# A second norm written out tile by tile over four k-steps, and a latent copied out of PSUM

## The chip, the cores and the metric

The kernel runs on one core of a Trainium2 chip. The metric is the time of one execution on the device in microseconds (us); of several executions the median is taken. The engines of the core run side by side and wait for each other by semaphores: TensorE (PE) multiplies and transposes into PSUM, VectorE (DVE) and ScalarE (ACT) work element by element, GpSimd (POOL) does a few small powers here, and the queue of SyncE (SP) issues the DMAs.

## The reference

Input is one sequence of 256 tokens of width 2048, in float32. A gMLP layer comes first, then one layer of latent attention, each with shift, scale and gate rows computed from a vector c (adaLN):

```python
h = rms_norm(x, norm_g[0]) * (1 + scale) + shift
u, v, z = jnp.split(h @ a_w_in, 3, axis=-1)
y = gelu(u) * mix(layer_norm(gelu(v))) * silu(z)
x = x + gate * (y @ a_w_out)                    # the projection: 4096 -> 2048
...
h_kv = rms_norm(x, kv_norm_g) * (1 + kv_scale) + kv_shift
c_kv, k_r = jnp.split(h_kv @ w_dkv, [512], axis=-1)   # block d: 512 + 64 columns
k_nope, v = heads(rms_norm(c_kv, g_kva) @ w_ukv)
k_rope = rope(rms_norm(k_r, g_kr))
...
h = rms_norm(x, norm_g[1]) * (1 + scale) + shift      # the second norm
c_q, z = jnp.split(h @ b_w_in, [512], axis=-1)        # blocks c (512 columns) and z, y (2 x 1024)
q = heads(rms_norm(c_q, g_qa) @ b_w_uq)
x = x + gate * ((attention(q, k, v) * silu(z)) @ b_w_out)
```

## The kernel before

The 256 tokens are two tiles of 128 (t = 0, 1). Every matrix product is a `Block`: per k-step a 1 MB piece of the weight comes by DMA into a slot of the pool `wraw` (4 slots, shared with the background rows below), and `load_split` splits each half of it into `hi`, a rounded copy made by ACT, and `lo`, the rest, made by DVE (pool `wsp`, 4 slots each). The other factor is split alike, so that a product is three matmuls: hi x hi, lo x hi and hi x lo. A k-step with 1024 columns is 2 halves x 2 tiles x 2 column halves x 3 = 24 matmuls of 512 columns. `drive` goes through the list of steps and issues the preparation of the next step ahead of the matmuls of this one.

`project()` (L630) multiplies with a_w_out in two Blocks of 16 k-steps each, for 1024 columns each. `ev_o` adds the gated result to x (`residual`, L624), and `norm1.chunk` sums the squares and transposes the row chunk into `zT`. In the last step of the second Block, `early1` (L688) runs for each tile: the mean's power on POOL (`rstd_of`, L136), one transpose to spread it over the partitions, the scaling of the first 4 of 16 chunks (L296), and their shift and scale to `h`, split into `gh` on ACT and `gl` on DVE. `late1` (L700) does the other 12 chunks for both tiles at once behind them.

Then `attention()` runs the blocks z and y (b_w_z, 8 k-steps each), d (kv_w_dkv, 8 steps, 288 + 288 columns) and c (b_w_q, 8 steps, 512 columns), all on `mm` banks of PSUM, and keys, queries and heads behind them. `ev_dkv` (L752) closes d: `latent_row` (L711) squares the latent out of PSUM on ACT, gets the power from POOL, and normalises it on ACT from PSUM into `cn`.

In the background the adaLN rows are made: `bg(quota)` adds the quota after each k-step and starts a row (`Ada.step`, L192: 1 MB by DMA into `araw`, one product over 2048 columns on DVE) whenever it has reached 1. The quota is AQ = 0.8 in the projection, until its step STOP = 14, and BQ = 0.9 in z and y, from z's step START = 2.

SP's queue holds the DMAs in the order of the program. The order on the other engines is made by the framework's scheduler, within the data's dependences; `behind(ins)` (L169) places an instruction after a given one.

## Time and profile before

| | us |
|---|---|
| median of 3 runs | 1130.31 |
| lowest, highest | 1128.52, 1131.99 |
| the profiled execution | 1135.89 |
| span of the profiled execution | 1134.2 |
| PE busy in it | 1103.1 |
| DVE busy in it | 952.4 |
| ACT busy in it | 618.4 |

All rows further down come from the profiled execution, whose mean granted TensorE clock was 0.991 of full speed. Its times count from the start of the span. Matmuls are pipelined: the duration of one in a row is longer than the distance to the next, and the distance is what counts. A name in a row is the program's name of a tile: `x` is the residual, `zT` the transposed chunk, `hi` and `lo` the weight's parts, `gh` and `gl` those of h in blocks z, y and c, `shi` and `slo` those in the projection and in d, `araw` a background row, `cn` the latent, `px`, `pm` and `pk` are PSUM tiles.

### The profile page before, as it was taken

What the parts mean: (1) busy time and instruction counts of PE and PEld (TensorE: products, weight loads), DVE (VectorE), ACT (ScalarE), POOL (GpSimd) and SP (SyncE); (2) the same over time, 40 slices, a digit from 0 to 9 for tenths busy, and PEclk for the clock granted to TensorE, in tenths of its full rate; (3) what the DMA queues carried; (4) which work ended last, traced back from release to release, by engine and by line L of the source; (5) the groups of instructions that cost most, each with busy time, mean ns of one, the idle gap of its engine ahead of it and who ended that gap; (6) DMA issues with size and microseconds to landing.
All of it is one profiled execution on the core that took longest, in us unless ns stands there. A gap on an engine that the chain in (4) does not pass through costs nothing.

```text
span 1134.2 us, 14344 instructions
## 1 busy us (share of the span) xinstructions
PE 1103.1 (97%) x5120; PEld 914.8 (81%) x5120; DVE 952.4 (84%) x1379; ACT 618.4 (55%) x1146; POOL 61.6 (5%) x79
## 2 busy tenths in 40 slices
PE   7989999999999999999999999989999999999998
PEld 4877788888888887888888888868889788898876
DVE  5789899989996896897799899869886658779995
ACT  6743445457854435444454455456737579885332
POOL 1000000000310000000000000000000024220000
PEclk8999999999999999999999999998999999999999
DMA  9997889898897988988979989967886645345893
GB/s 347 355 352 269 329 337 364 342 348 307 328 342 289 368 314 304 382 325 326 351 296 357 368 341 376 339 261 280 338 343 207 221 152 185 114 162 214 304 350 122
DMA packets 52330, 340.41 MB, mean 300 GB/s; under 512 B 5889, under 2 KB 6305, under 8 KB 13985
## 3 DMA queue, kind: packets, MB, share of 16 engines
q1 hardware_dynamic: 50402, 335.29, 79.1%
q10 hardware_dynamic: 1152, 2.10, 0.5%
q0 software_dynamic: 704, 2.11, 0.5%
q8 instruction: 40, 0.66, 0.2%
q14 instruction: 32, 0.26, 0.1%
HBM read 337.36 MB, written 2.11 MB: 299 GB/s over the span
## 4 chain that ended last, share of the span: by engine, by line
PE 75%; DVE 9%; DMA 8%; issue 4%; ACT 3%; POOL 0%; DVEq 0%; SPq 0%; ACTq 0%; POOLq 0%
PE pm L341 63%; DMA araw<-in_ada_wT 8%; PE pk L341 4%; DVE lo L167 4%; DVE araw L192 3%; PE pq L341 2%; PE pS L885 1%; PE pS L886 1%; ACT sq L146 1%; ACT hi L165 1%; PE pmix L581 1%; PE px L263 1%; DVE v L481 1%; DMA x<-in_x 0%; PE pT L903 0%
## 5 line engine op out<-in xcount | busy, mean ns | idle before, releaser
L165 ACT CAST hi<-raw 128x1024 fp32r<-128x1024 f32 (+2 forms) x376 | 381.4, 1030 | 379.8 <-PE pm L341 257.0
L167 DVE TENSOR_TENSOR lo<-raw,hi 128x1024 fp32r<-128x1024 f32 (+2 forms) x376 | 442.0, 1195 | 71.4 <-ACT hi L165 68.9
L192 DVE CUSTOM_DVE_ANT_0 araw<-araw,s_b,vec 128x2048 f32<-128x2048 f32 (+1 forms) x128 | 275.1, 2149 | 49.2 <-DMA araw<-in_ada_wT 45.6
L341 PE MATMUL pm<-lo,hh 128*128 128x512 f32 x768 | 249.6, 393 | 4.2 <-DVE lo L167 4.1
L341 PE MATMUL pm<-hi,hh 128*128 128x512 f32 x768 | 242.6, 394 | 8.0 <-ACT hh L302 3.5
L341 PE MATMUL pm<-hi,hl 128*128 128x512 f32 x768 | 247.1, 391 | 0.0
L341 PEld LDWEIGHTS pm<-hi,hh 128*128 128x128 f32 x768 | 144.1, 188 | 41.0 <-ACT hi L165 4.1
L341 PEld LDWEIGHTS pm<-lo,hh 128*128 128x128 f32 x768 | 144.0, 189 | 36.8 <-DVE lo L167 7.4
L341 PEld LDWEIGHTS pm<-hi,hl 128*128 128x128 f32 x768 | 144.6, 188 | 30.3
L341 PE MATMUL pm<-lo,shi 128*128 128x512 f32 (+1 forms) x320 | 94.9, 372 | 0.0
L341 PE MATMUL pm<-hi,slo 128*128 128x512 f32 (+1 forms) x320 | 93.4, 371 | 0.0
L341 PE MATMUL pm<-hi,shi 128*128 128x512 f32 (+1 forms) x320 | 91.1, 373 | 0.0
L341 PEld LDWEIGHTS pm<-hi,shi 128*128 128x128 f32 x320 | 58.2, 188 | 10.1
L341 PEld LDWEIGHTS pm<-lo,shi 128*128 128x128 f32 x320 | 58.3, 188 | 9.9 <-DVE lo L167 0.2
L341 PEld LDWEIGHTS pm<-hi,slo 128*128 128x128 f32 x320 | 58.0, 188 | 10.1
L341 PE MATMUL pm<-hi,gh 128*128 128x512 f32 x160 | 52.7, 404 | 3.1 <-ACT cn L718 2.3
L341 PE MATMUL pm<-hi,gl 128*128 128x512 f32 x160 | 53.4, 400 | 0.0
L341 PE MATMUL pm<-lo,gh 128*128 128x512 f32 x160 | 52.8, 399 | 0.0
L165 ACT CAST shi<-yT 128x512 fp32r<-128x512 f32 x32 | 19.8, 620 | 45.0 <-PE pm L341 44.9
L341 PE MATMUL pm<-hi,ybh 128*128 128x512 f32 x128 | 42.9, 398 | 1.4 <-ACT ybh L165 1.4
L341 PE MATMUL pm<-hi,ybl 128*128 128x512 f32 x128 | 43.1, 399 | 0.0
L341 PE MATMUL pm<-lo,ybh 128*128 128x512 f32 x128 | 43.0, 395 | 0.0
(182 smaller groups left out, 1254.7 us busy)
## 6 DMA issues: line engine op xcount, KB each, us to landing
araw<-in_ada_wT SPq DMA_DIRECT2D x96, 1024.0 KB, 6.8
raw<-in_a_w_in SPq DMA_DIRECT2D x96, 1024.0 KB, 6.9
raw<-in_a_w_out SPq DMA_DIRECT2D x32, 1024.0 KB, 7.2
araw<-in_kv_ada_wT SPq DMA_DIRECT2D x32, 1024.0 KB, 6.9
raw<-in_b_w_z SPq DMA_DIRECT2D x16, 1024.0 KB, 6.2
raw<-in_b_w_out SPq DMA_DIRECT2D x16, 1024.0 KB, 5.9
raw<-in_kv_w_ukv SPq DMA_DIRECT2D x8, 1024.0 KB, 5.0
raw<-in_b_w_uq SPq DMA_DIRECT2D x8, 768.0 KB, 5.0
```

Source lines behind the costliest of these rows:

```text
L146: nc.scalar.activation(j, src, AF.Square, scale=scale, accum_out=dst)
L165: nc.scalar.copy(hi, src)
L167: nc.vector.tensor_tensor(out=lo, in0=src, in1=hi.bitcast(F32), op=ALU.subtract)
L192: nc.vector.tensor_tensor_reduce(out=t[:, c], in0=t[:, c], in1=s_b[:, c], scale=1.0, scalar=acc, op0=ALU.mult, op1=ALU.add, accum_out=dst)
L263: nc.tensor.transpose(p[:, j * P:(j + 1) * P], self.xt[t][:, (q * 4 + j) * P:(q * 4 + j + 1) * P], ident)
L341: nc.tensor.matmul(ps[i][:, :widths[i]], lhsT=lt, rhs=rhs[:, offs[i]:offs[i] + widths[i]], start=(first and c == 0 and which == 0 and rhs ...
L481: nc.vector.tensor_tensor(out=p, in0=ps, in1=p, op=ALU.add)
L581: nc.tensor.matmul(pmix[:, j * 256:(j + 1) * 256], lhsT=wsh["T"][:, g, :], rhs=piece(vt[i], t, n)[:, j * 256:(j + 1) * 256], start=True, s ...
L885: nc.tensor.matmul(pS[:, c0:c1], lhsT=qT[:, j, t * P:(t + 1) * P], rhs=kT[:, j, 0:nk], start=True, stop=False)
L886: nc.tensor.matmul(pS[:, c0:c1], lhsT=qrT[:, t * P:(t + 1) * P], rhs=krT[:, j, 0:nk], start=False, stop=True)
```

## The change

- **The seam.** `early1` and the last step of the second projection Block give way to `passage()`, which covers the last two steps of the projection (14 and 15) and the first two of z, in one written order. A wrapper around the engines, `Engines.keep("order")`, places every instruction of ACT, DVE and PE after the one that was written before it; `keep("behind")` places the later ones after the last of these. Step 15's weight is cast first, and z's step 0 into two slots of its own (`zw0`, `zw1`). Then come the matmuls: tile 0 of steps 14 and 15, tile 1 of step 14 and the first columns of 15, tile 0's broadcast, tile 1's other columns, z's steps 0 and 1 for tile 0 with tile 1's broadcast between, and z's steps 0 and 1 for tile 1. Block z starts at step 2 afterwards.
- **Background rows.** STOP goes from 14 to 12: two rows less are started in the projection's end. BQ goes from 0.9 to 1.0: one row per step in z and y. From z's first weights to the first step of d, 13 rows of the latent's norm and one of the last gate are started, where before there are 11 and two; the other row of the last gate moves to the keys and queries.
- **late1.** The scaling of each further four chunks is placed behind the `gl` of the second chunk of the four before, where before all stand behind the last of `early1`.
- **The latent.** `latent_row` copies the latent (288 + 224 columns), and `ev_dkv` the rotary key (64), from PSUM to SBUF on DVE; squares, power and scaling follow from there (`normalise`). The same holds for the query latent (512 columns) after c. Block d has tail = 1: its last step runs tile by tile, and tile 0 is closed before tile 1's matmuls.

```diff
-BQ = 0.9
+BQ = 1.0
-STOP = 14
+STOP = 12
...
+class Engine:
+    def __init__(self, tc, engine):
+        self.tc, self.engine, self.last, self.mode = tc, engine, None, None
+    def __getattr__(self, name):
+        f = getattr(self.engine, name)
+        if not self.mode:
+            return f
+        def call(*args, **kw):
+            with self.tc.issue_after(self.last.ins) if self.last else nullcontext():
+                ins = f(*args, **kw)
+            if self.mode == "order":
+                self.last = ins
+            return ins
+        return call
+class Engines:
+    def __init__(self, tc):
+        self.sync, self.gpsimd = tc.nc.sync, tc.nc.gpsimd
+        self.scalar, self.vector, self.tensor = (Engine(tc, e) for e in (tc.nc.scalar, tc.nc.vector, tc.nc.tensor))
+    def keep(self, mode):
+        for e in (self.scalar, self.vector, self.tensor):
+            e.mode, e.last = mode, e.last if mode else None
...
-        with behind(chain.pop(0) if chain and queue[0] else None):
-            nc.vector.tensor_tensor(out=lo, in0=src, in1=hi.bitcast(F32), op=ALU.subtract)
+        rest(src, hi, lo)
+    def rest(src, hi, lo):
+        nc.vector.tensor_tensor(out=lo, in0=src, in1=hi.bitcast(F32), op=ALU.subtract)
-    hold, queue, chain = [None], [False], []
+    hold = [None]
...
-            yield from b.items(AQ, tail=TAIL, after=early1 if i else None, then=late1 if i else None, before=fetch, stop=STOP if i else 99)
+            if i == 0:
+                yield from b.items(AQ, tail=TAIL, before=fetch)
+            else:
+                yield from b.items(AQ, tail=2, stop=STOP, bare=True)
+                at["z"] = z_block(0)
+                yield passage(b, at["z"], fetch)
+    def passage(b, z, fetch):
+        n, wd = b.nkk - 2, b.widths
+        def prep():
+            got, raw = b.prepare(n)(), load(b.w, n + 1, b.n)
+            fetch()
+            return got, raw, load(z.w, 0, z.n)
+        def comp(got):
+            (wa, la), raw, begin = got
+            hi, lo = ([wsp.tile([P, 1, NB], F32R, tag=g, name=g) for _ in range(2)] for g in ("hi", "lo"))
+            wb = [(hi[c][:, 0, :], lo[c][:, 0, :]) for c in range(2)]
+            for c in range(2):
+                split(raw[:, c:c + 1, :], hi[c], lo[c])
+            lb = b.lhs(n + 1)
+            raw = load(z.w, 1, z.n)
+            at["h"] = h1 = H("g")
+            z0 = []
+            nc.keep("order")
+            for c in range(2):
+                s = slot(f"zw{c}", F32R)
+                z0.append((s[:, 0:NB], s[:, NB:2 * NB]))
+                split(begin[:, c], *z0[c])
+            mms(b.ps[0], 0, la, wa, wd, False, False)
+            mms(b.ps[0], 0, lb, wb, wd, False, True, True)
+            b.close(t=0)
+            mms(b.ps[1], 1, la, wa, wd, False, False)
+            mms(b.ps[1], 1, lb, wb, wd, False, True, [0])
+            r = norm1.rstd(0)
+            hi, lo = ([wsp.tile([P, 1, NB], F32R, tag=g, name=g) for _ in range(2)] for g in ("hi", "lo"))
+            z1 = [(hi[c][:, 0, :], lo[c][:, 0, :]) for c in range(2)]
+            for c in range(2):
+                nc.scalar.copy(hi[c], raw[:, c:c + 1, :])
+            rest(raw[:, 0:1, :], hi[0], lo[0])
+            rb = norm1.spread(r)
+            norm1.scale(0, EARLY, 0, P, rb)
+            mms(b.ps[1], 1, lb, wb, wd, False, True, [1])
+            p = norm1.turn(0, 2)
+            at0 = [[h1.at(w, k)[:, 0:P] for w in range(2)] for k in range(EARLY)]
+            at1 = [[h1.at(w, k)[:, P:S] for w in range(2)] for k in range(EARLY)]
+            hs = [norm1.high("1", k, at0[k][0], 0, P) for k in range(2)]
+            norm1.keep(0, rb)
+            norm1.flipped(0, 2, p)
+            b.close(t=1, ns=[0])
+            for k in range(2):
+                norm1.low(hs[k], *at0[k])
+            hs = [norm1.high("1", k, at0[k][0], 0, P) for k in range(2, EARLY)]
+            b.close(t=1, ns=[1])
+            b.ps = None
+            for k in range(2, EARLY):
+                norm1.low(hs[k - 2], *at0[k])
+            z.ps = [[bank("pm", "mm") for _ in z.widths] for _ in range(NT)]
+            mms(z.ps[0], 0, z.lhs(0), z0, wd, True, False)
+            p = norm1.turn(0, 3)
+            norm1.flipped(0, 3, p)
+            mms(z.ps[0], 0, z.lhs(1), z1[:1], wd, False, False)
+            r = norm1.rstd(1)
+            rest(raw[:, 1:2, :], hi[1], lo[1])
+            rb = norm1.spread(r)
+            norm1.scale(0, EARLY, P, S, rb)
+            mms(z.ps[0], 0, lambda c, w: z.lhs(1)(1, w), z1[1:], wd, False, False)
+            p = norm1.turn(1, 2)
+            for k0 in range(0, EARLY, 2):
+                hs = [norm1.high("1", k, at1[k][0], P, S) for k in (k0, k0 + 1)]
+                for k in (k0, k0 + 1):
+                    hold[0] = norm1.low(hs[k - k0], *at1[k])
+            norm1.keep(1, rb)
+            norm1.flipped(1, 2, p)
+            for j, w in enumerate((z0, z1)):
+                mms(z.ps[1], 1, z.lhs(j), w, wd, j == 0, False)
+            nc.keep("behind")
+            norm1.flip(1, 3)
+        return prep, comp, late1, "late"
...
-    def early1(t):
-        rb = norm1.finish(t)
-        if "h" not in at:
-            at["h"] = H("g")
-        h1 = at["h"]
-        chain.append(norm1.scale(0, EARLY, t * P, (t + 1) * P, rb))
-        norm1.keep(t, rb)
-        for k in range(EARLY):
-            hold[0] = norm1.h("1", k, h1.at(0, k)[:, t * P:(t + 1) * P], h1.at(1, k)[:, t * P:(t + 1) * P], t * P, (t + 1) * P)
-            if k == 1:
-                chain.append(hold[0])
-            norm1.h("1", k, h1.at(0, k), h1.at(1, k))
+            low = norm1.h("1", k, h1.at(0, k), h1.at(1, k))
+            if k % 4 == 1:
+                hold[0] = low
-        r = rms_rstd(pieces)
-            nc.scalar.activation(cn[:, o:o + n], p, AF.Identity, scale=r)
+            nc.vector.tensor_copy(cn[:, o:o + n], p)
+    def normalise(row):
+        nc.scalar.activation(row, row, AF.Identity, scale=rms_rstd([row]))
...
-        kr = ps[:, w:w + DR]
-        r = rms_rstd([kr])
-        nc.scalar.activation(kn[:, 0, :], kr, AF.Identity, scale=r)
+        nc.vector.tensor_copy(kn[:, 0, :], ps[:, w:w + DR])
+        normalise(cn)
+        normalise(kn[:, 0, :])
...
+        normalise(cn)
...
-            "z": z_block(0).items(BQ, start=START), "y": b.items(BQ), "d": Block(lhs_k, a["kv_w_dkv"][0], KD // 2, [288, 288], ev_dkv).items(),
+            "z": at["z"].items(BQ, start=START, skip=2), "y": b.items(BQ), "d": Block(lhs_k, a["kv_w_dkv"][0], KD // 2, [288, 288], ev_dkv).items(tail=1),
```

On PE, where the projection (`shi`, `slo`) ends and block z (`gh`, `gl`) begins, before. `px<-ident,x` are the transposes of the norm's chunks, `px<-ident,rs` is the broadcast of the norm's power:

```order
L341 MATMUL pm<-hi,slo 128x512
L263 MATMUL px<-ident,x_0_232 128x128 x8
L287 MATMUL px<-ident,rs_5833 128x128
L263 MATMUL px<-ident,x_1_233 128x128 x8
L341 MATMUL pm<-hi,gh_5838 128x512 x2
L341 MATMUL pm<-lo,gh_5838 128x512 x2
L287 MATMUL px<-ident,rs_5895 128x128
L341 MATMUL pm<-hi,gl_5840 128x512 x2
```

After, from the last matmul of the projection to tile 1's broadcast; `zw` are z's first weights:

```order
L69 MATMUL pm<-hi,slo 128x512
L69 MATMUL px<-ident,x_0_232 128x128 x4
L69 MATMUL pm<-zw_5774,gh_5770 128x512 x4
L69 MATMUL pm<-zw_5774,gl_5772 128x512 x2
L69 MATMUL pm<-zw_5777,gh_5770 128x512 x4
L69 MATMUL pm<-zw_5777,gl_5772 128x512 x2
L69 MATMUL px<-ident,x_0_232 128x128 x4
L69 MATMUL pm<-hi,gh_5770 128x512 x2
L69 MATMUL pm<-lo,gh_5770 128x512 x2
L69 MATMUL pm<-hi,gl_5772 128x512 x2
L69 MATMUL px<-ident,rs_5915 128x128
```

Before, both tiles' transposes and the first broadcast stand between the two products. After, tile 0's broadcast stands seven rows ahead of this piece, among tile 1's matmuls of the projection, and tile 1's behind 18 matmuls of z.

On DVE in block z, before, behind the scalings of the last chunks (L296); the `ISA` rows with 2048 columns are the products of the background rows:

```order
L296 TENSOR_TENSOR zT_235<-zT_235,zrb 128x1024 x2
L192 ISA araw,col_sck<-araw,s_b,vec 128x2048
L192 ISA col_sck 128x1
L167 TENSOR_TENSOR lo<-raw,hi 128x1024 x2
L303 TENSOR_TENSOR gl_5840<-h,gh_5838 128x256 x2
L196 SCALAR_TENSOR_TENSOR col_sck<-col_sck,vec 128x1
L167 TENSOR_TENSOR lo<-raw,hi 128x1024 x2
L192 ISA araw,col_shk<-araw,s_b,vec 128x2048
L192 ISA col_shk 128x1
L303 TENSOR_TENSOR gl_5840<-h,gh_5838 128x256 x2
```

After, behind the low parts (L198) of z's step 5:

```order
L344 TENSOR_TENSOR gl_5773<-h,gh_5771 128x256 x2
L223 ISA araw,col_sck<-araw,s_b,vec 128x2048
L223 ISA col_sck 128x1
L223 ISA araw,col_shk<-araw,s_b,vec 128x2048
L223 ISA col_shk 128x1
L223 ISA araw,col_sck<-araw,s_b,vec 128x2048
L223 ISA col_sck 128x1
L344 TENSOR_TENSOR gl_5773<-h,gh_5771 128x256 x2
L227 SCALAR_TENSOR_TENSOR col_sck<-col_sck,vec 128x1
L198 TENSOR_TENSOR lo<-raw,hi 128x1024 x2
L223 ISA araw,col_shk<-araw,s_b,vec 128x2048
```

Before, two low parts and two chunks of h stand between one background product and the next. After, the first three products stand in a row between the chunks 13 and 14 of h, and the two low parts of step 6 behind them.

On DVE, where d ends (c's weights: `lo`, 1024 columns; the latent's sums: `ss`, `rs`), before:

```order
L167 TENSOR_TENSOR lo<-raw,hi 128x1024
L303 TENSOR_TENSOR slo<-h,shi 128x256
L167 TENSOR_TENSOR lo<-raw,hi 128x1024 x2
L159 TENSOR_REDUCE ss_6959<-ss_6954 128x1
L140 TENSOR_SCALAR rs_6961<-ss_6959 128x1
L167 TENSOR_TENSOR lo<-raw,hi 128x1024
```

After:

```order
L198 TENSOR_TENSOR lo<-raw,hi 128x1024 x2
L829 COPY cn<-pm 128x288
L829 COPY cn<-pm 128x224
L873 COPY kn<-pm 128x64
L829 COPY cn<-pm 128x288
L829 COPY cn<-pm 128x224
L873 COPY kn<-pm 128x64
L198 TENSOR_TENSOR lo<-raw,hi 128x1024 x2
```

The six copies out of PSUM stand behind the low parts of c's first step; the sums and the power follow two low parts later.

## Rows read from the trace of the kernel before

**Rows 1.** The profile page, its first part (engine, busy us, share of the span, instructions) and its fourth (the chain that ended last, share of the span by engine).

```profile
PE 1103.1 (97%) x5120; PEld 914.8 (81%) x5120; DVE 952.4 (84%) x1379; ACT 618.4 (55%) x1146; POOL 61.6 (5%) x79
...
PE 75%; DVE 9%; DMA 8%; issue 4%; ACT 3%; POOL 0%; DVEq 0%; SPq 0%; ACTq 0%; POOLq 0%
```

**Rows 2.** Timeline of TensorE from the projection's last two k-steps to the start of the d block. Columns: start us, duration us, engine, line, operation, out<-in, shape, count, and in brackets the idle time before it and what ended it.

```profile
747.07 1.07 PE L341 MATMUL pm<-hi,shi 128*128 128x512 f32 x4
...
757.73 0.39 PE L341 MATMUL pm<-hi,slo 128*128 128x512 f32 x1
758.37 0.63 PE L263 MATMUL px<-ident,x 128*128 128x128 f32 x4 [0.26 <-DVE x L626]
759.57 0.63 PE L263 MATMUL px<-ident,x 128*128 128x128 f32 x4 [0.57 <-DVE x L626]
762.33 0.47 PE L287 MATMUL px<-ident,rs 128*128 128x128 f32 x1 [2.12 <-POOL rs L141]
762.59 1.91 PE L263 MATMUL px<-ident,x 128*128 128x128 f32 x8
765.32 1.22 PE L341 MATMUL pm<-hi,gh 128*128 128x512 f32 x2 [0.81 <-ACT gh L302]
...
772.47 1.09 PE L341 MATMUL pm<-hi,gh 128*128 128x512 f32 x4
...
855.45 0.29 PE L341 MATMUL pm<-hi,shi 128*128 128x288 f32 x1
```

**Rows 3.** The chain of waits from 735 to 800 us, four pieces of the part between the projection and the z block. Columns: start us, duration us, engine, what, line.

```profile
760.03 1.20 DVE x L626 x2
...
761.71 0.57 POOL rs L141
...
762.84 0.70 DVE zT L296
...
763.83 0.77 ACT h L301 x2
```

**Rows 4.** Table of stretches. Columns: from:to us, length, then for PE, PE's weight loads, DVE, ACT and POOL the busy us (and instructions), the granted TensorE clock, the DMA share, GB/s.

```profile
769.00:771.00 2.00, 2.00 (x6) 1.51 (x6) 1.84 (x4) 1.84 (x7) 0.00 (x0) 0.50 0.84 352
773.00:775.00 2.00, 2.00 (x11) 1.64 (x10) 2.00 (x2) 0.50 (x1) 0.00 (x0) 1.00 0.88 360
780.00:800.00 20.00, 20.00 (x90) 16.57 (x89) 19.17 (x26) 14.24 (x25) 0.00 (x0) 1.00 0.97 374
800.00:820.00 20.00, 20.00 (x90) 16.58 (x89) 17.28 (x22) 16.44 (x27) 0.00 (x0) 1.00 0.87 328
885.00:887.00 2.00, 2.00 (x8) 1.51 (x7) 0.53 (x3) 0.87 (x5) 0.54 (x1) 0.50 0.81 309
960.00:970.00 10.00, 8.75 (x58) 7.94 (x57) 7.96 (x24) 8.06 (x36) 3.55 (x3) 1.00 0.61 212
1070.00:1080.00 10.00, 8.60 (x43) 6.95 (x42) 9.87 (x23) 4.69 (x5) 0.56 (x1) 1.00 0.82 304
```

**Rows 5.** Groups of instructions of DVE and ACT, forms kept apart, from 747 to 860 us. Columns: line, engine, operation, names, shapes, count, busy us, mean ns of one, idle us before them and what ended it.

```profile
L167 DVE TENSOR_TENSOR lo<-raw,hi 128x1024 fp32r<-128x1024 f32 x34 | 40.9, 1221 | 7.5 <-ACT hi L165 7.4
L192 DVE CUSTOM_DVE_ANT_0 araw<-araw,s_b,vec 128x2048 f32<-128x2048 f32 x12 | 28.2, 2347 | 0.9 <-DMA araw<-in_kv_ada_wT 0.8
L303 DVE TENSOR_TENSOR gl<-h,gh 128x256 fp32r<-128x256 f32 x12 | 4.8, 417 | 0.0
...
L626 DVE TENSOR_TENSOR x<-x,xr 128x512 f32<-128x512 f32 x4 | 2.6, 683 | 0.0
...
L296 DVE TENSOR_TENSOR zT<-zT,px 128x512 f32<-128x512 f32 x2 | 1.4, 685 | 1.3 <-PE px L287 1.3
...
L165 ACT CAST hi<-raw 128x1024 fp32r<-128x1024 f32 x34 | 35.5, 1052 | 33.4 <-PE pm L341 28.6 <-DMA raw<-in_b_w_z 4.6
...
L146 ACT ACTIVATE sq<-x 128x512 f32<-128x512 f32 x4 | 2.5, 626 | 0.0
```

**Rows 6.** DMA issues on SP's queue and the cast on ACT that waits for one (timeline, columns as in rows 2); in the last row the DMA view of 742 to 743 us (what, count, KB each, us from issue to landing).

```profile
734.59 0.33 SPq L184 DMA_DIRECT2D araw<-in_kv_ada_wT  x1
...
742.46 8.68 SPq L322 DMA_DIRECT2D raw<-in_b_w_z  x4
...
751.55 2.22 ACT L165 CAST hi<-raw 128x1024 fp32r<-128x1024 f32 x2 [2.21 <-DMA raw<-in_b_w_z]
...
raw<-in_b_w_z SPq DMA_DIRECT2D x1, 1024.0 KB, 9.0
```

**Rows 7.** Timeline of PE and ACT where the d block ends and the c block begins (columns as in rows 2).

```profile
880.45 0.69 PE L341 MATMUL pm<-hi,slo 128*128 128x288 f32 x4
883.42 0.50 PE L341 MATMUL pm<-hi,gh 128*128 128x512 f32 x1 [2.28 <-ACT cn L718]
...
887.37 0.43 PE L341 MATMUL pm<-hi,gh 128*128 128x512 f32 x1
...
880.78 0.41 ACT L146 ACTIVATE sq<-pm 128x288 f32<-128x288 f32 x1
...
882.87 0.84 ACT L718 ACTIVATE cn<-pm,rs 128x288 f32<-128x288 f32 x2 [0.32 <-POOL rs L141]
```

**Rows 8.** Two single prices from the keys: two transposes in the chain of waits of 912 to 925 us (start, duration, what), and DVE's copies of 256 columns out of PSUM in the groups of 880 to 945 us (columns as in rows 5).

```profile
918.33 0.22 PE px L828 x2
...
L822 DVE COPY pair<-pk 128x256 f32<-128x256 f32 x7 | 2.9, 419 | 0.6 <-ACT sq L146 0.5
```

More of the change, by code (lines that the diff above doesn't have):

```diff
@@ L334, in mms @@
         offs = [sum(widths[:i]) for i in range(len(widths))]
-        for some in ([[i] for i in range(len(widths))] if apart else [range(len(widths))]):
+        for some in ([[i] for i in (range(len(widths)) if apart is True else apart)] if apart else [range(len(widths))]):
             for c, (hi, lo) in enumerate(wt):
@@ L357, in drive @@
             if nxt and not late:
-                queue[0] = True
                 ready = nxt[0]()
-                queue[0] = False
             cur[1](got)
             if nxt and late:
-                queue[0] = True
                 ready = nxt[0]()
-                queue[0] = False
+                nc.keep(None)
             cur[2]()
@@ L390, in compute, with close @@
             return f
-        def close(self, evac=None, t=None):
+        def close(self, evac=None, t=None, ns=None):
             for t_ in range(NT) if t is None else (t,):
-                for i, wd in enumerate(self.widths):
+                for i in range(len(self.widths)) if ns is None else ns:
+                    wd = self.widths[i]
                     (evac or self.evac)(t_, i, self.ps[t_][i][:, :wd])
@@ L397, in close, with items @@
                 self.ps = None
-        def items(self, quota=0.0, tail=0, after=None, before=None, then=None, start=0, stop=99, at_step={}):
+        def items(self, quota=0.0, tail=0, before=None, start=0, stop=99, skip=0, bare=False, at_step={}):
             n = self.nkk - tail
-            for kk in range(n):
+            for kk in range(skip, n):
                 def post(kk=kk):
@@ L409, in items @@
                 yield self.prepare(kk), self.compute(kk), post
-            if tail:
+            if tail and not bare:
                 kks = range(n, self.nkk)
@@ L423, in comp @@
                         self.close(t=t)
-                        if after:
-                            after(t)
                 def post():
-                    if then:
-                        then()
                     bg(quota * tail if n < stop else 0.0)
-                yield (prep, comp, post, "late") if then else (prep, comp, post)
+                yield prep, comp, post
     norm0 = Norm(xt, "x")
```

31 lines of the change are left out of this document (21 added, 10 removed).

## The prediction

> **What bounds the kernel now.** I read the page's first and fourth parts first: TensorE (PE) is busy 97% of the span and holds 75% of the chain that ended last, VectorE (DVE) 84% [rows 1]. So time is only won where PE stands still or runs slowly, and those places are few. The timeline of PE around the second norm shows the largest one [rows 2]: the projection's last matmul starts at 757.73, and the first of the z block at 765.32. [...] The chain of waits names what stands in the gap: residuals on DVE, the mean's power on POOL, the scaling on DVE, h on ACT [rows 3]. The second place is the end of the d block: PE idles 2.28 us until ACT's normalisation of the latent has left PSUM, and is slow afterwards [rows 7]; the clock of 885 to 887 was 0.50 [rows 4].
>
> **What the seam costs before.** The 48 matmuls from 747.07 to 757.73 follow each other every 0.227 us [rows 2], so a k-step of 24 takes 5.45 us. From 747.07 to the first matmul of d at 855.45 [rows 2] lie 108.4 us. Two projection steps and sixteen of z and y are 432 matmuls, 98.0 us at 0.227. The 18 transposes of the norm cost 0.11 each at full clock, as two of them elsewhere take 0.22 [rows 8]: 2.0 us. So 8.4 us are lost in this stretch. Their places: the last matmul is over at 757.96, so the gap is 7.36 us, of which 17 transposes (1.87) are work: 5.5 lost. From 765.32 to 772.47 there are 18 matmuls and one transpose, 7.15 us where 4.2 would do: 2.9 lost. 5.5 + 2.9 = 8.4, so nothing else is lost there.
>
> **Part 1: the seam, tile by tile (-8.4, then +1.4).** The work stays the same in number; its order changes, and PE has matmuls of tile 1 to do while tile 0 is normalised. I laid the new order out by hand with the durations of [rows 5] and of the chain [rows 3], each instruction starting when its engine and its inputs are free, from 747.07 on. Tile 0's 24 matmuls end at 752.5. DVE does the last casts' low parts until 752.0 (1.22 each [rows 5], a little overlapped), then the four residual operations of tile 0 until 754.5; ACT's two sums of squares end at 755.3, POOL's power (0.57, [rows 3]) at 756.2. PE asks for it at 756.6, after 18 matmuls of tile 1: no wait, where 2.1 us were waited before. Scaling (0.69) after one queued low part, h and its cast are ready at 759.1; PE has finished tile 1 and four transposes at 758.6: 0.5 us of wait. Tile 1 repeats this behind z's first 18 matmuls: 0.06 us at its broadcast. The chunks 4 and 5 of h, made for both tiles at once, cost 0.5 and 0.35 more. Together 1.4 us. None of these waits comes near the 1.25 us (960 to 970) and 1.4 us (1070 to 1080) of idle time in which the clock stayed at 1.00 [rows 4], so I count no slow matmuls. The bounds of this term: nothing, if the chunks come early; and 1.4 + 2.9 = 4.3, if the clock falls all the same.
>
> This rests on z's first weights being there. Before, their load is issued at 742.46, behind a background load at 734.59, takes 9.0 us, and ACT waits 2.21 for it until 751.55 [rows 6]. STOP = 12 takes two of the background loads out of the queue, and z's load moves up to about 735; with 9.0 us it lands at 744. Nor do the two products of 2.35 us [rows 5] then stand in DVE's queue. What if it comes late is the third rival.
>
> **Part 2: what that pushes into the z block (+2.1, +1.7).** The two background rows come back later, and BQ = 1.0 asks for one row per k-step instead of 0.9. The held order and late1's rule that a scaling follows the h of the chunk before put all h chunks up to 13 ahead of the first background product on DVE; then three products stand in a row, ahead of the low part of z's step 6 (the order of DVE after, in the section on the change). By the laid-out schedule the products start at 788.0, when the last low part of step 5 and two chunks are done. Three of 2.35 are 7.05, two chunks of 0.42 make 0.8, and the low part takes 1.22 [rows 5]: it is ready at 797.1. PE wants it at 795.0. So PE waits 2.1 us in front of step 6's second pair of matmuls. This is close to the 2.28 us idle of [rows 7] after which the clock fell, and further from the 1.25 and 1.4 that left it at 1.00; so I take the fall and its price there, below: 1.7 us. Both ends: 0 if the products slip apart, 2.1 + 1.7 = 3.8 as taken.
>
> From step 4 of z on, twelve steps load 2.10 MB each (a weight tile and a background row) in 5.45 us: 385 GB/s. The highest rate in these blocks is 374 GB/s at a DMA share of 0.97 [rows 4]; at that rate a step takes 5.61 us, and the twelve 1.9 us more, less what is loaded ahead. I take 0, as four slots hold one step and more ahead, and keep 1.9 for the range. DVE has 2 x 1.22 + 2.35 = 4.8 us of work per step of y: it fits.
>
> [...]
>
> **Part 3: the latent leaves PSUM by copies (-4.0).** Before, the c block waits for a PSUM bank that ACT holds: squares at 880.78, another cast, the normalisation from 882.87, and c starts at 883.42 after 2.28 us idle. Until 887.37 there follow nine matmuls and two transposes in 3.95 us; at full clock 9 x 0.227 + 0.22 = 2.26. So the slow clock took 1.7 us [rows 7], and the whole 4.0. After, three DVE copies per tile free the banks, and tail = 1 closes tile 0 half a step (1.6 us) ahead of d's end. A copy of 256 columns out of PSUM takes 0.42 [rows 8]; 288 and 224 columns are then about 0.45 and 0.4, estimated from it. Behind at most one low part of 1.22 the first bank is free at about 880.5, and c can start at 881.1. Normalisation moves behind c's matmuls, which last 25 us. Bounds: 0 (if two low parts stand ahead of the copies) to 4.0. I take 4.0.
>
> [...]
>
> **The rest.** One row of 2.35 us for the last gate moves from z/y into the keys and queries, and that stage is ordered anew. ACT, not PE, has little slack there. I count 0, bounds -1.5 to +1.5, from PE's idle of 1.25 us in the one stretch of it [rows 4]. The output projection stays as it is. Start to 747 is unchanged.
>
> **Sum.** -8.4 + 1.4 + 2.1 + 1.7 - 4.0 = -7.2. The profiled execution took 1135.89 us (span 1134.2); the median of the runs is 1130.31, 0.5% less, so this profile is a slow sample. On it I expect 1128.7, and on the median **1123.1 us**.
>
> **The rivals.**
> - *No pile-up at step 6:* the products spread, or the idle time leaves the clock at 1.00. Then 1.7 to 3.8 us less: 1119.3 to 1121.4. For it: the schedule's margin is one instruction of DVE. Against: the order puts the three products in one row.
> - *The copies come late:* DVE is in low parts when d ends, c waits as before. 1123.1 + 4.0 = 1127.1. For it: two low parts of c's weights stand directly ahead of the copies. Against: half a step of lead.
> - *z's first weights come late:* if their load still waits until 742.46, all three engines wait in their held order. Low parts move from 752.0 to 754.9, so PE waits 2.9 us at the first broadcast and the clock falls (2.0 or so): 1128.0. Against: the queue ahead is shorter by two.
> - *The loads set the pace (slower):* with one row per step, every held-up row blocks DVE's queue, and behind it the next step's low parts. At the 328 GB/s of 800 to 820 [rows 4] a step takes 6.39 us, 0.94 more, over twelve steps 11.3: 1134.4. It decides from 331 GB/s down (10.6 us lost) that the kernel is slower, and between 331 and 364 (3.8 lost) that nothing changes. For it: 328 is a row of this block. Against: the DMA share was 0.87 there, so that was what was asked for, and 374 at 0.97.
>
> **How the numbers follow.** Three runs cannot tell less than about 0.3% (3.4 us) from no change, so faster is below 1126.9 and slower above 1133.7. Forecast (1121.4 to 1126) 0.50; no pile-up 0.18; copies late 0.09; weights late 0.06; loads set the pace 0.17, of which 0.08 within 0.3% and 0.09 slower. Faster is 0.50 + 0.18 = 0.68, same 0.09 + 0.06 + 0.08 = 0.23, slower 0.09. The range takes the forecast with its bounds, the pile-up's absence with 1.5 us of the rest, and goes up over the late copies and the late weights: 1118 to 1129.5, with about 0.15 outside.
>
> **What would show it.** Right: PE goes from projection to z with no idle time over 0.6 us and the clock at 1.00 from 750 to 790; one wait of about 2 us on a low part some 47 us after the start of projection step 14, behind three background products; c starts within 0.3 us of d's end. Wrong: a DMA releasing ACT's first z cast; clock under 1.00 in the seam; a wait of PE on DVE in every step of y; a wait in front of c. The sum fails if the keys and queries lose more than 1.5 us.

## The result: slower by a quarter of a per cent

| | before | after |
|---|---|---|
| median of 20 runs each, us | 1132.06 | 1135.78 |
| lowest, highest | 1128.52, 1137.42 | 1129.03, 1140.47 |
| ratio after / before | | 1.0028, 95% interval 1.0014 to 1.0041 |
| the profiled execution, us | 1135.89 | 1134.64 |
| its span | 1134.2 | 1132.9 |

The two spans alone would say that the change wins 1.3 us. They can't be compared so: PE's instructions up to the projection's step 14 are the same in every kernel of this study, yet step 14 starts between 741.99 and 748.39 us in the profiled executions (747.07 before, 741.99 after). STOP isn't the reason: the seven kernels with STOP = 12 alone spread from 741.99 to 747.13. So all lengths below count from the first matmul of step 14, and end with the last matmul. From there to the end it is 381.7 us before and 385.6 after, 3.8 more, which fits the 3.7 between the medians.

Timeline of PE after, at the places that answer to [rows 2] and [rows 7]. L69 is the line of the wrapper that holds the order, so it stands for the whole seam:

```profile
741.99 0.62 PE L69 MATMUL pm<-hi,shi 128*128 128x512 f32 x2
...
751.71 0.32 PE L69 MATMUL px<-ident,rs 128*128 128x128 f32 x1
...
754.33 1.20 PE L69 MATMUL pm<-zw,gh 128*128 128x512 f32 x4 [0.47 <-ACT gh L69]
...
760.32 0.32 PE L69 MATMUL px<-ident,rs 128*128 128x128 f32 x1 [1.14 <-POOL rs L170]
...
769.24 0.73 PE L386 MATMUL pm<-hi,gh 128*128 128x512 f32 x2 [0.79 <-ACT gh L340]
...
805.55 0.99 PE L386 MATMUL pm<-hi,gh 128*128 128x512 f32 x2 [2.35 <-ACT szb L853]
...
849.25 0.29 PE L386 MATMUL pm<-hi,shi 128*128 128x288 f32 x1
...
874.84 0.47 PE L386 MATMUL pm<-hi,gh 128*128 128x512 f32 x1
```

The first broadcast has no wait, z starts 12.3 us after step 14 where it was 18.25, and c starts (874.84) without a gap. The seam and the end of d do what the change says. The table of stretches after answers to [rows 4] (columns as there):

```profile
742.00:760.00 18.00, 16.68 (x76) 12.98 (x74) 14.98 (x24) 11.82 (x25) 1.69 (x2) 1.00 0.38 144
760.00:800.00 40.00, 38.51 (x172) 31.39 (x173) 34.51 (x45) 29.45 (x55) 0.26 (x1) 1.00 0.68 249
...
870.00:880.00 10.00, 9.97 (x60) 8.90 (x59) 7.38 (x16) 6.84 (x15) 1.61 (x4) 1.00 0.66 187
897.00:1016.00 119.00, 115.03 (x634) 101.87 (x633) 87.38 (x262) 95.17 (x378) 31.73 (x32) 0.97 0.44 155
```

The clock is 1.00 in the seam and at d's end, where it had fallen to 0.50 before [rows 4]. It is now 0.97 over the 119 us of keys, queries and heads. There the time has gone. Lengths from the start times of PE's rows (output begins with the first matmul on `ybh`):

| us | step 14 to z | z to d | d to c | c to keys | keys to output | output to end | sum |
|---|---|---|---|---|---|---|---|
| before | 18.3 | 90.1 | 28.0 | 24.8 | 112.0 | 108.6 | 381.7 |
| after | 12.3 | 94.9 | 25.6 | 22.9 | 118.4 | 111.4 | 385.6 |
| difference | -5.9 | +4.8 | -2.4 | -1.8 | +6.4 | +2.7 | +3.8 |

So 1.1 us are won up to d and 4.2 with the latent, and 9.2 lost behind them, in a stage of which the change rewrites nothing but the query latent. What PE waits for from the keys on, before (columns: engine, line and releaser; us in total, times, longest):

```profile
PE pm L341 <- ACT ybh L165: 1.4, 1, 1.4
PE px L828 <- ACT kt L827: 1.4, 2, 1.2
```

and after:

```profile
PE px L943 <- ACT kt L942: 2.7, 4, 1.0
PE pm L386 <- ACT ybh L194: 1.9, 2, 1.5
PE pm L386 <- DVE ybl L198: 1.4, 2, 0.8
PE pT L1018 <- DVE pair L978: 0.8, 1, 0.8
```

With the small ones the waits are 3.3 us before and 7.2 after. The rest is the clock. PE after, where the queries begin:

```profile
917.55 0.27 PE L943 MATMUL px<-ident,kt 128*128 128x128 f32 x1
917.65 0.60 PE L840 MATMUL px<-ident,cn 128*128 128x128 f32 x4
918.09 0.27 PE L943 MATMUL px<-ident,kt 128*128 128x128 f32 x1
919.15 0.33 PE L943 MATMUL px<-ident,kt 128*128 128x128 f32 x1 [0.79 <-ACT kt L942]
919.68 0.84 PE L943 MATMUL px<-ident,kt 128*128 128x128 f32 x3 [0.20 <-ACT kt L942]
920.70 0.53 PE L386 MATMUL pq<-hi,latq 128*128 128x384 f32 x1 [0.18 <-ACT latq L194]
```

For 3.2 us PE does ten transposes and waits three times; then the clock is at half. It falls a second time behind the waits for `pair` and `kt` (0.80 and 1.04 us, at 960). One stretch of 2 us from each fall:

```profile
921.00:923.00 2.00, 2.00 (x8) 2.00 (x8) 1.17 (x5) 1.13 (x5) 0.00 (x0) 0.50 0.30 122
...
963.00:965.00 2.00, 2.00 (x6) 1.52 (x6) 1.93 (x9) 1.92 (x9) 0.00 (x0) 0.50 0.03 8
```

Summed over such stretches (2 us times what the clock lacks to 1.00) each of the two falls costs 1.7 us, 3.4 together; before, there is none behind the keys. 3.9 us of waits and 3.4 of clock are 7.3 of the 9.2; the other 1.9 are spread over small gaps that I did not place.

### The profile page after: what moved, and what is told of

It is laid out like the page before. It is cut to its first block, busy times and chain, and to the rows that moved or that the text cites. A ratio compares the mean times of both kernels' runs of the same rounds, so it can differ in the third digit from the quotient of the medians.

```text
span 1132.9 us, 14359 instructions
## 1 busy us (share of the span) xinstructions
PE 1103.7 (97%) x5120; PEld 913.3 (81%) x5120; DVE 955.7 (84%) x1385; ACT 616.8 (54%) x1140; POOL 62.9 (6%) x79
## 4 chain that ended last, share of the span: by engine, by line
PE 76%; DVE 9%; DMA 7%; ACT 5%; issue 3%; POOL 0%; DVEq 0%; SPq 0%; ACTq 0%; POOLq 0%
PE pm L386 66%; DVE araw L223 3%; DMA araw<-in_ada_wT 3%; PE pk L386 3%; DVE lo L198 3%; PE pq L386 2%; ACT hi L194 2%; DMA raw<-in_a_w_in 1%; PE pmix L620 1%; ACT sq L175 1%; PE pm L69 1%; DMA raw<-in_b_w_z 1%; DMA raw<-in_b_w_out 1%; PE pt L627 1%; DVE sz L520 0%
## 5 line engine op out<-in xcount | busy, mean ns | idle before, releaser
L194 ACT CAST hi<-raw 128x1024 fp32r<-128x1024 f32 (+2 forms) x370 | 374.3, 1029 | 374.4 <-PE pm L386 264.1
L198 DVE TENSOR_TENSOR lo<-raw,hi 128x1024 fp32r<-128x1024 f32 (+2 forms) x370 | 435.3, 1195 | 84.2 <-ACT hi L194 82.1
L386 PE MATMUL pm<-lo,shi 128*128 128x512 f32 (+1 forms) x304 | 89.3, 371 | 0.0
L386 PE MATMUL pm<-hi,slo 128*128 128x512 f32 (+1 forms) x304 | 89.2, 370 | 0.0
L386 PE MATMUL pm<-hi,shi 128*128 128x512 f32 (+1 forms) x304 | 85.6, 371 | 0.0
L386 PEld LDWEIGHTS pm<-lo,shi 128*128 128x128 f32 x304 | 55.1, 188 | 9.2 <-DVE lo L198 0.2
L386 PE MATMUL pm<-hi,gh 128*128 128x512 f32 x144 | 46.4, 393 | 3.2 <-ACT szb L853 2.4
L386 PE MATMUL pm<-lo,gh 128*128 128x512 f32 x144 | 47.5, 391 | 0.4 <-DVE lo L198 0.4
L386 PE MATMUL pm<-hi,gl 128*128 128x512 f32 x144 | 47.1, 390 | 0.0
L386 PE MATMUL pk<-hi,latkv 128*128 128x512 f32 x128 | 43.9, 411 | 0.0
```

The costliest lines, as they stand in the source:

```text
L194: nc.scalar.copy(hi, src)
L198: nc.vector.tensor_tensor(out=lo, in0=src, in1=hi.bitcast(F32), op=ALU.subtract)
L386: nc.tensor.matmul(ps[i][:, :widths[i]], lhsT=lt, rhs=rhs[:, offs[i]:offs[i] + widths[i]], start=(first and c == 0 and which == 0 and rhs ...
```

## The experiments

All ratios are to the kernel before on the same chip, with 95% intervals. "Order" is how much of PE's rows from the first key matmul on stands in the same sequence as in the kernel before (1.00: all; the changed kernel 0.76). The framework's scheduler makes this order. "Sum" is the time from step 14 to the end.

### The parts alone

e1_seam_only takes the latent back:

```diff
+        r = rms_rstd(pieces)
-            nc.vector.tensor_copy(cn[:, o:o + n], p)
+            nc.scalar.activation(cn[:, o:o + n], p, AF.Identity, scale=r)
...
-        normalise(cn)
...
-[288, 288], ev_dkv).items(tail=1)
+[288, 288], ev_dkv).items()
```

> The changed kernel with the latent as before (normalised out of PSUM on ScalarE, the last step of d not split by tiles); the seam, STOP = 12 and BQ = 1.0 stay. Measured from the start of projection step 14, the changed kernel is 1.3 us ahead at d, 5.5 ahead at the keys, and 3.7 behind at the end, so it loses 9 us in keys, queries, heads and output. Theory A (the loss comes with the order that the scheduler gives this stage, which the seam and the background rows set off): the stage still loses about 9 us, d to c has its 4 us back, the total is about 7.5 us over the kernel before, ratio 1.005 to 1.008. Theory B (the loss comes with the copies and the later normalisation of the latent): no loss in the stage, total 1 us or so under before, ratio 0.997 to 1.001.

Measured: ratio 1.0031 (1.0014 to 1.0049); keys to end 226.6 us, 6.0 more than before; c waits 2.6 us again; order 0.78. The ratio lies between the ranges of the two theories: 6.0 of the 9 us are left without the copies, and the changed kernel's stage is 3.2 longer, with two falls of the clock where this one has one. e2_copies_only is the kernel before with the same lines put in.

> The kernel before with only the latents' copies and the last step of d split by tiles; seam, STOP = 14 and BQ = 0.9 as before. Theory A: the stage of keys and queries keeps its length of before (112 us from the first key matmul to the first output matmul, within 1.5), c starts within 0.3 us of d's end, the total is about 4 us less, ratio 0.995 to 0.998. Theory B: the stage becomes 5 us or more longer, ratio 1.002 to 1.006.

Measured: ratio 0.9983 (0.9969 to 0.9998); keys to end 220.8 us, 0.15 more than before; order 0.98. Theory B is out: in the kernel before the copies leave the stage alone, and the seam with its rows brings most of the loss. But c still waits:

```profile
879.33 0.50 PE L341 MATMUL pm<-hi,gh 128*128 128x512 f32 x1 [1.17 <-DVE cn L717]
```

The copies stand behind a low part on DVE there, so 2.9 us are won in place of 4.2. e3 and e5 change one thing each in the changed kernel:

```diff
-BQ = 1.0
+BQ = 0.9
```

> The changed kernel with BQ = 0.9 in place of 1.0. Theory A: the stage of keys and queries is ordered anew (its order is nearer to the one of before), so its length changes by more than 2 us against the changed kernel, and the wait in front of y (2.35 us, ScalarE's cast of y's first weights waiting for its load) gets shorter, since a row less is loaded; ratio to before 0.995 to 1.000. Theory B: the stage stays as long as in the changed kernel; only the z block gains, up to 2.7 us; ratio 1.000 to 1.003.

Measured: ratio 1.001 (0.9991 to 1.0029); order 0.87; the wait in front of y 1.07 us, which can't be put down to BQ, as e1, with BQ = 1.0, has 0.84. Keys to output became 3.5 us shorter than in the changed kernel, output 3.4 longer, with one fall of the clock in each: another order, as bad a one (229.7). How near an order is to the one of before doesn't measure its loss.

```diff
-            if k % 4 == 1:
-                hold[0] = low
```

> The changed kernel with all further scalings of late1 placed behind the last chunk that the seam makes, as before, in place of one after the other. The stage of keys and queries keeps the order of the changed kernel, so both theories leave its length as it is there, within 1 us. It asks for the pile-up in z: if three background products in a row ahead of step 6 are what makes the loads of steps 6, 7 and y late (they free their slots late), the waits of 0.4 and 2.35 us in z go, ratio 1.000 to 1.002; if the loads' rate alone does it, the wait in front of y stays, ratio 1.002 to 1.004.

Measured: ratio 1.0068 (1.0042 to 1.0094). Neither case came about. The wait in front of y is gone, but the products now stand ahead of the chunks, and PE waits for those (waits of PE in the seam, z and y):

```profile
PE pm L386 <- ACT gh L340: 2.5, 1, 2.5
PE pm L386 <- DVE gl L344: 2.4, 1, 2.4
```

The line is needed: it keeps the chunks ahead of the products. And it pushes all three products behind chunk 13, the last that it holds, as each product is placed behind `hold[0]`. The copies of the latent come late here too (c waits 1.17 us). The stage kept its order, and PE had the same waits in it before the output projection, but it took 227.6 us, 2.2 less than in the changed kernel, as neither of the two falls of the clock came.

### One background row

The row of the last gate that falls into keys and queries stands ahead of the first queries in the changed kernel, and behind the fourth pair before. f1 moves it back by a number, f2 moves it forward in the kernel before (`+ 0.8`):

```diff
-ev_q).items(BQ2)}
+ev_q).items(BQ2, at_step={0: lambda: quota.__setitem__(0, quota[0] + -0.8)})}
```

> The changed kernel with one number more: 0.8 is taken off the background quota after the first step of c, so that the one gate row in keys and queries is started behind the fourth pair of blocks, as in the kernel before, and no longer ahead of the first queries. The order that the scheduler gives the stage is then close to that of before (0.96 of TensorE's rows in common sequence, against 0.76 in the changed kernel). Theory C (the row's place sets the order of the stage, and the order costs the 9 us): keys to end falls from 229.8 us to within 3 us of the 220.6 of before, ratio to before 0.994 to 0.998. Theory D (the stage loses because it is entered earlier and in another state, wherever the row is): it stays above 226, ratio 1.000 to 1.003.

Measured: ratio 0.9979 (0.9956 to 1.0003); keys to end 222.1 us where the changed kernel has 229.8, with the waits of before on the keys:

```profile
PE px L943 <- ACT kt L942: 1.4, 2, 1.2
PE pm L386 <- DVE ybl L198: 1.1, 1, 1.1
PE pm L386 <- ACT ybh L194: 0.7, 1, 0.7
```

> The kernel before with 0.8 added to the background quota after the first step of c: the gate row in keys and queries comes ahead of the first queries, as in the changed kernel, and the order of the stage becomes nearly the changed kernel's (0.97 of TensorE's rows in common sequence). Seam, latent and all else as before. Theory C: the same loss as in the changed kernel arises, keys to end 226 to 231 us where before has 220.6, ratio 1.005 to 1.009, with a fall of the clock of 1.7 us in it. Theory D: no change beyond 2 us, ratio 0.998 to 1.002.

Measured: ratio 1.004 (1.0019 to 1.0061); keys to end 225.6 us, 5.0 more than before and just under the range of theory C, with one fall of the clock (1.7 us) and new waits:

```profile
PE px L828 <- ACT kt L827: 1.7, 2, 1.0
```

One number takes 7.7 us out of the changed kernel's stage and puts 5.0 into that of before. Theory D is out. But the number moves more than one row. The quota runs on, so every later row starts earlier or later with the first: four rows start between c's first and the output's first matmul in the changed kernel and in f2, three in the kernel before and in f1. And a row of the last gate is four products of 0.75 us on DVE, not one of 2.35. Between the first key and the first output matmul there are 14 of them in the changed kernel (10.4 us of DVE) and 12 in f2 (9.0), against 8 before (6.0) and 9 in f1 (6.7). One place where they cost time can be read in f2 (DVE and PE):

```profile
960.74 0.75 DVE L192 CUSTOM_DVE_ANT_0 araw<-araw,s_b,vec 128x512 f32<-128x512 f32 x1 [0.30 <-DMA araw<-in_ada_wT]
...
961.41 0.49 DVE L863 COPY pair<-px 128x128 f32<-128x128 f32 x2
...
961.76 0.55 PE L903 MATMUL pT<-ident,pr 128*128 128x128 f32 x3 [0.71 <-DVE pair L863]
...
963.35 0.72 PE L828 MATMUL px<-ident,kt 128*128 128x128 f32 x2 [1.04 <-ACT kt L827]
```

DVE waits for the row's load, makes a product, and only then the copies that PE waits for. In the kernel before no product stands there; PE has one wait of 1.25 us at this place and the clock stays at 1.00. In f2 the two waits are 1.75 us together, and the fall of the clock (1.7 us) comes behind them.

f4 is the kernel before with `STOP = 12` and `BQ = 1.0` alone; f3 the changed kernel with `STOP = 14` and `BQ = 0.9`.

> The kernel before with only STOP = 12 and BQ = 1.0. The order of keys and queries becomes that of the changed kernel (0.97). Theory C: keys to end 226 to 231 us, ratio 1.004 to 1.010; seam and latent as before. Theory D: the stage stays within 2 us of 220.6. For the z and y blocks: if one row per step is more than the loads can bring (385 GB/s), TensorE waits there by 1 us or more without any seam; if the waits in z come from the pile-up that the held order makes, there are none.

Measured: ratio 1.0051 (1.0027 to 1.0075); keys to end 228.0 us, order 0.78. In z and y PE waits 0.3 us in all, and the loads bring 389 GB/s in 780 to 800:

```profile
780.00:800.00 20.00, 20.00 (x90) 16.57 (x89) 19.91 (x26) 14.49 (x24) 0.00 (x0) 1.00 0.99 389
```

So one row per step is not more than the loads can bring while nothing holds them up; the waits in z come with the seam and its held order.

> The changed kernel with STOP = 14 and BQ = 0.9, so that the background rows are started where before starts them; the order of keys and queries is then 0.99 that of before. Theory C: the seam's gain and the copies' remain and the stage is as before: from projection step 14 to the end 370 to 375 us against 381.7 before, ratio 0.992 to 0.996, unless z's first weights come late behind the two rows that are back in the queue, which would cost up to 3 us at the seam. Theory D: the stage still loses 5 us or more, ratio 0.998 to 1.001.

Measured: ratio 0.9963 (0.9939 to 0.9988), faster than both kernels; keys to end 220.9 us as before, order 0.99. The ratio is just over theory C's range, and the sum is 376.5 us, 1.5 above the range, as the seam waits 2.2 us at the first broadcast: a background product (2.35 us) is scheduled in the middle of tile 0's residual on DVE.

```profile
757.18 0.32 PE L69 MATMUL px<-ident,rs 128*128 128x128 f32 x1 [2.17 <-POOL rs L170]
```

### Towards a better version

g1: `STOP = 13`, `BQ = 0.9`, quota - 0.2; g2: `BQ = 0.95`, quota - 0.1; g3: f3 with the hold ending at chunk 9; g4: g1 with it.

```diff
-            if k % 4 == 1:
+            if k % 4 == 1 and k <= 9:
                 hold[0] = low
```

> The changed kernel with STOP = 13, BQ = 0.9 and 0.2 taken off the background quota after c's first step, so that one row fewer stands in front of z than in f3_old_rows and the gate row of keys and queries keeps the place of before. In f3 a background product of 2.35 us stands between tile 0's residual operations on VectorE and TensorE waits 2.2 us at the first broadcast. If that product is the whole reason, the wait goes and the seam's z starts 12.3 us after step 14 as in the changed kernel; keys to end as before within 3 us (theory C); from step 14 to the end 373 to 377 us, ratio 0.990 to 0.996. If z's weights were late by themselves, the wait stays at 1 us or more.

Measured: ratio 0.9954 (0.9936 to 0.9972), sum 375.8; z again 12.3 us after step 14. z's first weights are issued 8.3 us ahead of step 14 in both, so the product was the reason and not the weights.

> The changed kernel with BQ = 0.95 and 0.1 off the quota after c's first step; STOP = 12 as there. Seam as in the changed kernel (12.3), gate row behind the fourth pair as before, so theory C has keys to end at 220 to 224 us. In z and y the rows stand between the 0.9 of e3 (1.07 us of wait in front of y) and the 1.0 of the changed kernel (2.35). End 374 to 378 us after step 14, ratio 0.991 to 0.997. Theory D: 226 or more from keys to end.

Measured: ratio 0.9965 (0.9949 to 0.9982), sum 376.5, keys to end 222.1; 1.08 us of wait in front of y.

> f3_old_rows with the hold of late1 ending at chunk 9: background products in z may start behind chunk 9 in place of chunk 13, so that two of them stand there and the others spread between later chunks. Order of keys and queries as in f3. If the row of three products behind chunk 13 makes the waits in the z block, those of step 6 and after (0.38 and 0.29 us in f3) go and nothing else changes: end 375 to 376.5, ratio 0.993 to 0.998. If products ahead of chunks 10 to 13 only move the wait to the chunks, as in e5, a wait of 1 us or more on chunk 10 or 11 appears: end 377 to 380.

Measured: ratio 0.9943 (0.9927 to 0.996), sum 375.8. The waits at and behind step 6 are gone, none has come on a chunk; but 0.4 is new in front of y, where f3 has none.

> g1 and g3 together: STOP = 13, BQ = 0.9, 0.2 off the quota, hold ending at chunk 9. Best case: no wait at the first broadcast, none in z from step 6 on, keys to end as before: end 372 to 374.5 us after step 14, ratio 0.988 to 0.994. If products at chunk 9 hurt, it is slower than g1 by 1 us or more.

Measured: ratio 0.9925 (0.9908 to 0.9943), sum 375.3: the lowest ratio of all, 8 us by the medians (1125.65 against 1133.74), though its interval overlaps those of g3 and h1. The sum missed the range (374.5) by 0.8; output to end is 110.6, 2 more than before.

> g4 with one instruction of VectorE moved: the low part of the second half of z's step 1 (1.22 us, two operands from SBUF) stands ahead of tile 0's last two chunks, no longer right behind tile 1's mean. In the changed kernel and in g4, POOL's power for tile 1 takes 1.39 us where the one for tile 0 takes 0.56, and TensorE waits 1.14 us at tile 1's broadcast, where the prediction had 0.06. Theory S (POOL's instruction is held while VectorE's low part runs beside it): the power takes 0.55 to 0.6 us, the wait falls to 0.2 to 0.5 us, the z block begins its step 2 0.6 to 0.9 us earlier. Theory L (the second power is long by itself, or since it comes 7 us after the first): it stays at 1.4 us and the wait within 0.2 us of 1.14. The total moves by under 1 us, so ratio to before 0.990 to 0.995 by either; the profile decides.

Measured: ratio 0.9928 (0.9902 to 0.9954); POOL's power takes 0.55 us and PE waits 0.30:

```profile
761.06 0.55 POOL L170 TENSOR_TENSOR rs<-rs,nhalf 128x1 f32<-128x1 f32 x1 [7.22 <-DVE rs L69]
...
761.66 0.32 PE L69 MATMUL px<-ident,rs 128*128 128x128 f32 x1 [0.30 <-POOL rs L170]
```

Theory S holds. z's step 2 starts 26.4 us after step 14 in place of 27.3, and the 0.8 us are given back in front of y (1.14 us of wait there, 0.21 in g4): the load of y's first weights is issued 0.8 earlier, and ACT still has them no sooner (56.2 us after step 14, 56.0 in g4).

## Why the prediction was wrong

**The seam: right in mechanism, the waits too small.** The 5.5 us of gap and 2.9 of slow matmuls went, and nothing waits at the first broadcast, as laid out; z's first weights were in time. The term 1.4 measured 2.4 (0.47, 1.14, 0.79), and about 3.5 with the slow start behind each wait (the distances between matmuls there are some 0.3 us longer than the wait explains). What failed in this term is the second broadcast, 0.06 predicted. POOL's two powers after, and what DVE does beside the second:

```profile
751.09 0.56 POOL L170 TENSOR_TENSOR rs<-rs,nhalf 128x1 f32<-128x1 f32 x1 [123.49 <-DVE rs L69]
758.87 1.39 POOL L170 TENSOR_TENSOR rs<-rs,nhalf 128x1 f32<-128x1 f32 x1 [7.22 <-DVE rs L69]
...
758.64 1.22 DVE L69 TENSOR_TENSOR lo<-raw,hi 128x1024 fp32r<-128x1024 f32 x1
```

I took the 0.57 of [rows 3], where DVE was idle. Started 0.2 us behind the beginning of a low part, the power takes 1.39 us and ends 0.4 behind the low part; in h1, where that low part runs earlier, it takes 0.55, so the neighbour makes the difference. I gave the power one length in both places and didn't weigh what runs beside it. Which of the two starts first goes with it here: tile 0's power, too, has a low part beside it, but one that starts 0.4 us later, and it took 0.56. By what means the one holds up the other, no run shows.

**The z block: the pile-up was right, its victim wrong.** Predicted 2.1 us of wait at step 6 and 1.7 of clock, 3.8. Measured 0.38 there, since PE came later itself, no fall, and 2.35 in front of y, with the slow start about 3.7 in all. The size fits by luck: from z to d it is 94.9 us here, but 93.3 in e1 and 96.6 in f1 (with a fall of the clock, 0.59 and 0.56 in 811 to 815), which have the same rows and the same seam. How the three products reach y (DVE, SP, ACT after; last the time of that load from issue to landing):

```profile
783.74 2.35 DVE L223 CUSTOM_DVE_ANT_0 araw<-araw,s_b,vec 128x2048 f32<-128x2048 f32 x1
...
786.01 2.35 DVE L223 CUSTOM_DVE_ANT_0 araw<-araw,s_b,vec 128x2048 f32<-128x2048 f32 x1
...
788.28 2.35 DVE L223 CUSTOM_DVE_ANT_0 araw<-araw,s_b,vec 128x2048 f32<-128x2048 f32 x1
...
791.30 2.36 DVE L198 TENSOR_TENSOR lo<-raw,hi 128x1024 fp32r<-128x1024 f32 x2
...
793.68 0.33 SPq L361 DMA_DIRECT2D raw<-in_b_w_z  x1
...
801.59 2.00 ACT L194 CAST hi<-raw 128x1024 fp32r<-128x1024 f32 x2 [3.21 <-DMA raw<-in_b_w_z]
803.61 1.28 ACT L853 ACT_TABLE_LOAD   x1
804.90 1.09 ACT L853 ACTIVATE szb<-pm 128x512 f32<-128x512 f32 x2
...
raw<-in_b_w_z SPq DMA_DIRECT2D x1, 1024.0 KB, 7.8
```

The products put off step 6's low part to 793.66; only then is a slot of `wraw` free for y's first weights, whose load is issued at 793.68 and takes 7.8 us. ACT casts them ahead of the silu that empties z's PSUM banks, with a table load between. PE gets its banks at 805.55. I followed DVE and PE there, and not ACT's queue behind the late load.

That the load is issued late comes from the pile-up: f4, with the same rows and no held order, issues it 48.9 us after step 14, where it is 51.7 here, and waits 0.3 us in all of z and y; but PE also comes to y 3.0 us later there (63.7 us after step 14, 60.7 here), so f4 doesn't say what the pile-up costs. Nor does the late issue set the size of the wait. In the changed kernel, f1, e1, e3 and g2 the load is issued at the same 51.7 us, behind the same three products; it takes 7.8, 7.9, 6.2, 6.4 and 6.4 us, and PE waits 2.35, 2.35, 0.84, 1.07 and 1.08. In g1 it is issued at 51.7 too, ACT has it 5.5 us later, and PE waits 0.17. PE is at y at the same time in all six (60.7 to 60.8). What decides between 5.5 and 7.9 us stays open. g3 and g4 don't show that earlier products cure this wait: f3 and g1, from which they differ in the hold alone, wait no longer (0 and 0.17 us against 0.41 and 0.21); PE is at y 1.3 and 0.7 us sooner in g3 and g4. What the table of stretches shows is that little is loaded while the products hold the slots (180 GB/s, a DMA share of 0.43), and that the DMA engines are fully busy right behind (0.99):

```profile
781.00:783.00 2.00, 2.00 (x11) 1.65 (x10) 1.81 (x3) 1.97 (x4) 0.00 (x0) 1.00 0.43 180
784.00:802.00 18.00, 17.62 (x79) 14.26 (x77) 17.89 (x22) 8.93 (x17) 0.00 (x0) 1.00 0.99 363
```

So the rival of loads that set the pace was wrong for the twelve steps as a whole, as f4's 389 GB/s show, but in the steps behind the pile-up the loads do set when y can start.

**The latent: right.** -4.0 predicted, -4.2 measured (2.4 from d to c, 1.8 in c). The margin was thinner than the text says: in e2 and e5 the copies come behind one more low part, and 1.17 us of the wait are back. Nor is the 1.7 us of clock in this term a fixed price: in f4 PE waits 2.17 us at this place and the clock stays at 1.00.

**"The rest": the step that failed.** "I count 0, bounds -1.5 to +1.5" measured +9.2; the prediction's last sentence had named this as the way its sum would fail. I knew that the stage is ordered anew, and took its bounds from one wait of PE. But an order isn't a wait: the whole stage of 220 us, which PE nearly fills, is laid out again, and after the change it has eleven waits of 0.2 to 1.5 us where it had five, and two falls of the clock of 1.7 us between them. What set it off was named beside it, the row of the last gate that moves: f1, f2 and f4 show that the rows' places carry 5.0 to 7.7 us. The sentence on the row was wrong too: it took one row of 2.35 us, and the change brings six more products of 0.75 us ahead of the output, as the rows behind it move up. With this term at its value, -7.2 becomes +2.0; with the seam's 2.1 more, and 0.1 and 0.2 less in z and the latent, it is the measured +3.8. The forecast of the median was low by another 1.8 us, as its base of three runs (1130.31) was: 20 runs of the kernel before give 1132.06.

Left open: how much of the loss is the rows' own work beside keys and queries, and how much the order that the scheduler makes around it. At one place, f2's at 960, the products themselves are seen in front of PE's wait: 0.5 us more of it than before, and a fall of the clock behind it. Beyond that the two could not be parted. In the kernels of this study they go together: the six with four rows ahead of the output take 114.9 to 118.4 us from keys to output, the nine with three take 112.0 to 112.2. e3, whose order is another and whose loss is as great, has four as well (13 products, 9.7 us), and 16 rows of the last gate behind c where there are 14 before and 15 after; so it doesn't speak for the order alone. The falls of the clock don't follow from the order either: e5, in the changed kernel's order, had none, e1 and f4, close to it, one each.

## What to carry to other kernels

- Where a scheduler orders the program, a change to one stage must be read in the orders of all later stages. If a tuned stage comes out in another order, give it a loss, not zero (here 2 to 4% of its length), or bring the thing that moved back to its place first: here one number was worth 7.7 us. Count the background work that each stage gets before and after, too.
- A work item that is put off must be followed through the slot that it frees, up to the load, the cast and whatever stands behind that cast on its engine.
- Align two traces at an instruction that both share before subtracting; the spans alone had the wrong sign here.

## What the hardware showed that I had not expected

- A one-column power on POOL takes 1.39 to 1.40 us beside VectorE's 1.22 us subtraction of two SBUF tiles where it starts 0.2 us behind it (tile 1's power in the changed kernel, e1, f3, g4). It takes 0.55 us without it (tile 1's in h1), and 0.56 where the subtraction starts 0.4 us behind the power (tile 0's in all of these).
- The length of PE's idle time alone didn't tell here whether the clock falls. The same wait of 2.35 us in front of y left it at 1.00 in the changed kernel (805 to 807) and was followed by 0.59 in f1_row_back, 811 to 813 (the changed kernel's stretch, then f1's wait and stretch):

```profile
805.00:807.00 2.00, 1.45 (x5) 1.02 (x6) 2.00 (x3) 2.00 (x5) 0.00 (x0) 1.00 1.00 422
```

```profile
810.76 1.20 PE L386 MATMUL pm<-hi,gh 128*128 128x512 f32 x2 [2.35 <-ACT szb L853]
...
811.00:813.00 2.00, 2.00 (x5) 1.41 (x5) 1.58 (x2) 2.00 (x5) 0.00 (x0) 0.59 1.01 414
```

At 918 to 921 waits of 0.79, 0.20 and 0.18 us between transposes preceded a fall; in e5 the same three waits at the same place did not. So the prediction's reasoning, no fall where no wait comes near 1.25 or 1.4 us, gave no bound. The cost of a fall was the same 1.7 us for both falls of the changed kernel and for those of f1 (811 to 815), f2 and f4 (963 to 969).
